# Sixteen-row loads in three buffers, and the last store ahead of the waits for all other transfers, in a row-mean kernel

## The chip, the core and the metric

The kernel runs on one core of a Trainium2 chip. The metric is the device time of one execution in microseconds (us). The span in a profile is shorter, by 1.6 us for the kernel before: it ends with the core's last instruction and leaves out the exit that follows. All runs told here have the state "fast" (none is over 1.5% above the fastest of its kernel), unless the text says otherwise, and the granted clock was 1.0 in every one.

## The reference

```python
x = randn(32, 512, 1024)            # float32, 64 MiB
out = np.sum(x, axis=-1) / 1024.0   # float32, 32 x 512
```

There are 16,384 rows of 4 KB, 128 per SBUF partition, each read once and reduced to one number.

## The kernel before

Rows are loaded in bulk by the sync engine (SP), summed by VectorE with some help from ScalarE, and scaled. The first 16 rows of each partition and the next 96 are scaled by GpSimd and stored; the last 16 are summed and scaled in small pieces, so that little is left to do when the last bytes land.

```python
    first = [(2, 0), (14, 0)]                      # rows of a load, rows of it on ScalarE
    main = [(14, 0)] * 5 + [(14, 4), (12, 5)]
    last = [(9, 4), (4, 2), (2, 1)]                # and one row in two halves, pa and pb
    ...
    bulk = ctx.enter_context(tc.tile_pool(name="bulk", bufs=3))
    ...
            t = bulk.tile([P, 14, D], F32, name="t")
            load(t[:, :rows, :], src[:, j : j + rows, :])
            ...
            nc.vector.reduce_sum(out=dst[:, j : j + d], in_=t[:, :d, :], axis=AX)
        ...
        nc.gpsimd.tensor_scalar_mul(out=dst, in0=dst, scalar1=scale)
    ...
    tc.keep_in_program_order(nc.sync.dma_start(out=o_main, in_=res))    # the large store, 96 rows
    ...
    dve_mean(fin[:, j:], pb)                                            # the last mean
    tc.keep_in_program_order(nc.sync.dma_start(out=o_last, in_=fin))    # the last store
```

After scheduling, a helper edits how the program closes. `drain` stands for the sync engine's waits for every transfer and engine, `end.instructions[1:-1]` for the closing barrier of all engines (two rounds; between them GpSimd clears the semaphores), and `last` for the wait for the last store's landing:

```python
    end.instructions = [
        with_sync(drain, on_wait=tuple(needs.values())),        # all but VectorE's last mean
        with_sync(store, on_wait=(done,), on_update=(add,)),    # VectorE's last mean
        *end.instructions[1:-1],
        with_sync(last, on_update=(sub,)),
    ]
```

## Time and profile before

| | before |
|---|---|
| median time, 6 runs | 160.75 us (160.63 to 160.82) |
| span of the profile | 159.1 us |
| DMA engines busy / VectorE busy | 98.2% / 74% |
| last half row lands | 157.13 us |
| last store issued / landed | 157.62 / 159.02 us |

The prediction shows the lines that give the bound (the last line of its first block, on the last store, stands in the view of DMA issues and not on the page). The timeline (start, duration, engine, line, operation) shows the last mean and the last store:

```profile
157.50 0.08 DVE L164 DVE_READ_ACCUMULATOR2_ANT fin<- 128x1 f32 x1
157.62 0.33 SPq L200 DMA_DIRECT2D out_dram<-fin  x1
```

The view of line L231, where the closing instructions stand, gives for each kind its count, its shortest, median and longest duration in ns, and its first and last start:

```profile
L231 SPq EVENT_SEMAPHORE  x7: 17/27/28, 155.9 to 158.8; - x7
L231 POOLq EVENT_SEMAPHORE  x4: 17/17/17, 158.2 to 158.7; - x4
...
L231 SPq DRAIN  x3: 7/7/129, 157.5 to 158.4; - x3
```

The sync engine begins its waits at 155.9, before the last store. GpSimd (POOLq) leads the barrier: it has everyone's first report at 158.2 and gives the last release at 158.7.

### The profile page before, as it was taken

The page shows a single profiled execution, that of the slowest core. Times are in us where ns is not written, and L with a number is a line of the kernel's source. Part 1 is how long each engine was busy: PE and PEld are TensorE (multiplying, and loading weights), DVE is VectorE, ACT ScalarE, POOL GpSimd, SP SyncE. Part 2 cuts the span into 40 slices and gives each one's busy share as a digit, 9 for nine tenths or more (in the row PEclk, how much of TensorE's full clock was granted, in tenths as well). Part 3 has the DMA queues.
Part 4 walks back from the last instruction along what each step waited for, and adds up shares of the span by engine and source line. Part 5 has one row for each costly group of instructions (what it writes and reads, how often), then busy time and mean ns, then how long its engine had stood idle before and what let it go on. Part 6 is the DMA issues. An engine that isn't in the chain of part 4 may idle for free.

```text
span 159.1 us, 147 instructions
## 1 busy us (share of the span) xinstructions
DVE 117.2 (74%) x29; ACT 18.5 (12%) x33; POOL 1.0 (1%) x7
## 2 busy tenths in 40 slices
DVE  0500059995999599977999599959995996395643
ACT  3000000000000000000000000000000900390684
POOL 0000000000000000000000000000000000001000
DMA  8999999979999999789999999699999999999894
GB/s 303 422 461 461 461 461 461 433 317 404 461 461 461 461 461 461 317 375 461 461 461 461 461 461 418 303 433 461 461 461 429 396 396 445 445 445 445 375 406 159
DMA packets 2448, 67.18 MB, mean 422 GB/s; under 512 B 656, under 2 KB 656, under 8 KB 912
## 3 DMA queue, kind: packets, MB, share of 16 engines
q1 hardware_dynamic: 2448, 67.18, 98.2%
HBM read 67.11 MB, written 0.07 MB: 422 GB/s over the span
## 4 chain that ended last, share of the span: by engine, by line
DMA 77%; DVE 21%; SPq 1%; issue 0%; DVEq 0%
DMA t<-in_x_dram 56%; DMA pb<-in_x_dram 21%; DVE res L177 20%; SPq L154 1%; DVE pb L164 0%; DVEq L231 0%
## 5 line engine op out<-in xcount | busy, mean ns | idle before, releaser
L177 DVE TENSOR_REDUCE res<-t 128x14 f32<-128x14336 f32 (+3 forms) x9 | 111.2, 12360 | 34.1 <-DMA t<-in_x_dram 34.1
L158 ACT ACTIVATE junk<-t 128x1024 f32<-128x1024 f32 x16 | 16.2, 1013 | 136.9 <-DMA t<-in_x_dram 136.9
L164 DVE CUSTOM_DVE_ANT_0 t<-t 128x512 f32<-128x512 f32 x8 | 5.1, 690 | 6.1 <-DMA t<-in_x_dram 6.1
L158 ACT ACTIVATION_READ_ACCUMULATOR junk<-t 128x1 f32 x16 | 3.0, 187 | 0.0
L179 POOL TENSOR_SCALAR res<-res 128x16 f32<-128x16 f32 (+1 forms) x2 | 0.7, 352 | 143.3 <-DVE res L177 143.3
L158 ACT ACT_TABLE_LOAD x1 | 1.3, 1283 | 1.7 <-PEq L217 1.7
L164 DVE DVE_READ_ACCUMULATOR2_ANT fin<- 128x1 f32 x9 | 0.8, 83 | 0.0
L164 DVE CUSTOM_DVE_ANT_0 pb<-pb 128x257 f32<-128x257 f32 x1 | 0.4, 428 | 0.2 <-DMA pb<-in_x_dram 0.2
L164 DVE CUSTOM_DVE_ANT_0 pa<-pa 128x256 f32<-128x256 f32 x1 | 0.4, 426 | 0.0
L151 POOL MEMSET pb<- 128x2 f32 x1 | 0.1, 99 | 1.3 <-POOLq L217 1.3
L217 POOL MEMSET const-bfloat16-1.0<- 128x1 bf16 x1 | 0.1, 102 | 0.0
L217 POOL MEMSET const-uint8-127<- 128x1 uint8 x1 | 0.1, 101 | 0.0
L217 POOL MEMSET const-float32-0.0<- 128x1 f32 x1 | 0.1, 98 | 0.2 <-issue 0.2
L217 POOL MEMSET const-float32-1.0<- 128x1 f32 x1 | 0.1, 98 | 0.0
L164 DVE DVE_READ_ACCUMULATOR2_ANT pb<- 128x1 f32 x1 | 0.1, 84 | 0.0
## 6 DMA issues: line engine op xcount, KB each, us to landing
t<-in_x_dram SPq DMA_DIRECT2D x7, 7168.0 KB, 35.6
t<-in_x_dram SPq DMA_DIRECT2D x1, 6144.0 KB, 33.3
t<-in_x_dram SPq DMA_DIRECT2D x1, 4608.0 KB, 27.2
t<-in_x_dram SPq DMA_DIRECT2D x2, 1024.0 KB, 19.2
t<-in_x_dram SPq DMA_DIRECT2D x1, 2048.0 KB, 31.7
pa<-in_x_dram SPq DMA_DIRECT2D x1, 256.0 KB, 33.9
pb<-in_x_dram SPq DMA_DIRECT2D x1, 256.0 KB, 33.9
out_dram<-res SPq DMA_DIRECT2D x1, 48.0 KB, 11.6
```

What stands on the lines that cost most here:

```text
L151: nc.gpsimd.memset(pb[:, D - c :], 0.0)
L154: tc.keep_in_program_order(nc.sync.dma_start(out=dst, in_=src))
L158: nc.scalar.activation(junk, src, COPY, scale=by, accum_out=dst)
L164: nc.vector.tensor_tensor_reduce(out=src[:, :h], in0=src[:, :h], in1=src[:, h:], scale=by, scalar=0.0, op0=ADD, op1=ADD, accum_out=dst,)
L177: nc.vector.reduce_sum(out=dst[:, j : j + d], in_=t[:, :d, :], axis=AX)
L179: nc.gpsimd.tensor_scalar_mul(out=dst, in0=dst, scalar1=scale)
L217: nc = _bacc.Bacc("TRN2", target_bir_lowering=False, num_devices=1)
```

## The change

Its intent: fewer and larger loads (64 KB a partition instead of 56), so one load fewer, with a four-row tile given up to make room for three larger buffers; and a last store that waits for nothing but its own data, its lane (the semaphore that its landing would raise in the scheduled program, shared with an earlier transfer) and the engines that make it, with the waits for everything else behind it.

```diff
     end.instructions = [
+        with_sync(store, on_wait=store.sync_info.on_wait, on_update=(add,)),
         with_sync(drain, on_wait=tuple(needs.values())),
-        with_sync(store, on_wait=(done,), on_update=(add,)),
         *end.instructions[1:-1],
 ...
-    main = [(14, 0)] * 5 + [(14, 4), (12, 5)]
+    main = [(16, 0)] * 4 + [(16, 4), (16, 7)]
 ...
-    t4 = one.tile([P, 4, D], F32, name="t4")
     t2 = one.tile([P, 2, D], F32, name="t2")
-    pa = one.tile([P, 768], F32, name="pa")[:, :c]
+    pa = one.tile([P, c], F32, name="pa")
 ...
-            t = bulk.tile([P, 14, D], F32, name="t")
+            t = bulk.tile([P, 16, D], F32, name="t")
 ...
-        t = bulk.tile([P, 14, D], F32, name="t")[:, :rows, :] if rows > 4 else t4 if rows == 4 else t2
+        t = t2 if rows == 2 else bulk.tile([P, 16, D], F32, name="t")[:, :rows, :]
```

## The prediction

> **What bounds the kernel now.** I read the page first, then the groups by shape, the timeline, the chain of waits and the sync engine's own waits. The page says which engine has no room:
>
> ```profile
> DVE 117.2 (74%) x29; ACT 18.5 (12%) x33; POOL 1.0 (1%) x7
> ...
> q1 hardware_dynamic: 2448, 67.18, 98.2%
> ...
> out_dram<-res SPq DMA_DIRECT2D x1, 48.0 KB, 11.6
> ...
> out_dram<-fin SPq DMA_DIRECT2D x1, 8.0 KB, 1.4
> ```
>
> VectorE is idle for a quarter of the span, while the 16 DMA engines hold packets for 98.2% of it. The page's row of GB/s jumps between 303 and 461; I don't read that as stalls, since a slice is some 4 us and one 56 KB packet takes 2.1 us, so a slice is credited with one packet per engine more or less. The landings tell the rate better, and in the timeline each reduction starts when its load has landed:
>
> ```profile
> 21.60 15.09 DVE L177 TENSOR_REDUCE res<-t 128x14 f32<-128x14336 f32 x1 [14.60 <-DMA t<-in_x_dram]
> ...
> 38.51 15.09 DVE L177 TENSOR_REDUCE res<-t 128x14 f32<-128x14336 f32 x1 [1.83 <-DMA t<-in_x_dram]
> ...
> 106.19 15.09 DVE L177 TENSOR_REDUCE res<-t 128x14 f32<-128x14336 f32 x1 [1.83 <-DMA t<-in_x_dram]
> ...
> 123.15 10.82 DVE L177 TENSOR_REDUCE res<-t 128x10 f32<-128x10240 f32 x1 [1.87 <-DMA t<-in_x_dram]
> ...
> 137.71 7.62 DVE L177 TENSOR_REDUCE res<-t 128x7 f32<-128x7168 f32 x1 [3.75 <-DMA t<-in_x_dram]
> ```
>
> From 38.51 to 123.15 there are five loads of 14 rows (7,168 KB, 7,340,032 bytes): 84.64 / 5 = 16.93 us each, 433.6 GB/s. VectorE waits about 1.8 us before each. A late buffer would show as a longer gap between two landings, and there is none. The chain of waits in order of time shows how it ends:
>
> ```profile
> 106.19 15.10 DVE res L177
> ...
> 121.30 0.33 SPq L154
> ...
> 123.19 33.94 DMA pb<-in_x_dram
> ...
> 157.15 0.43 DVE pb L164
> ```
>
> The 15.10 us of VectorE in that chain are there because a load's issue waited for a buffer, not because the DMA ran dry: the load issued at 121.30 queued behind one that landed at 137.71. So the bound is bytes through the DMA engines, plus a tail after the last half row has landed at 157.13: 0.45 us of VectorE, a store issued at 157.62, 1.4 us to its landing, span 159.1. The sync engine's waits give the tail's slack:
>
> ```profile
> SPq L231 <- DMA pa<-in_x_dram: 0.6, 1, 0.6
> ...
> SPq L231 <- DMA pb<-in_x_dram: 0.6, 1, 0.6
> ...
> SPq L87 <- SPq L87: 0.3, 1, 0.3
> ```
>
> The first two are waits ahead of the last store. The third is the final wait for that store's landing: only 0.3 us, so the closing barrier (L231), which runs while the store is in flight, is nearly as long as the store itself.
>
> **What the Trainium skill says.** Three places bear on it. "DMA: Bandwidth & Descriptors", section "Where 436 GB/s comes from", gives 435.2 GB/s for the 16 ports; the 433.6 found here is 99.6% of it, so there is almost nothing to win. "HBM Reference", section "Specifications (TRN2)", says that a core streaming alone gets about 425 GB/s rather than its half of the pair's 716; this trace agrees, slightly above. The first page's section "Anatomy of one DMA" gives a fixed cost of about 2.0 us per DMA (for the GpSimd path). Here that holds only for a transfer that someone waits for (1.4 us for the last store). For a load with another behind it the trace disagrees: 7,340,032 bytes at 435.2 GB/s are 16.87 us, and a load takes 16.93, so 0.06 us is all that comes on top.
>
> **The change part by part.** *One load fewer.* The packet records in the trace have one packet per partition row of a load, eight per engine: 57,344 bytes take 2,116 ns, 36,864 bytes 1,364 ns, 8,192 bytes 309 ns. From the first and the last, the slope is 1,807 / 49,152 = 0.03676 ns a byte (27.2 GB/s an engine, 435 for 16) and the rest is 309 - 301.2 = 7.8 ns per packet. The bytes stay. The 96 main rows go in six loads instead of seven, so eight packets per engine vanish: 8 x 7.8 = 62 ns. I estimate a 64 KB packet at 65,536 x 0.03676 + 7.8 = 2,417 ns and a 16-row load at 8 x 2,417 = 19.34 us. The saving is on the path: -0.06 us.
>
> *Do the larger buffers still arrive in time?* Loads land at 21.6, then each 19.34 us: 40.9, 60.3, 79.6, 98.9, 118.3, 137.6; nine rows, 10.85 us, 148.5; four, 4.86, 153.4; two, 2.50, 155.9; the halves, 157.07. A reduction over 16 rows: 14 take 15.085 and 7 take 7.620 us, so 1.066 a row and 0.16 fixed, 17.2 us, below 19.34. The load landing at 98.9 needs the buffer of that from 40.9: free at 58.1, while one load that lands at 60.3 and another at 79.6 are still queued, 21 us in hand. The four-row load, now in a bulk buffer, waits for the load of 118.3: VectorE's 12 rows take 12.95 us, to 131.2 (ScalarE's four rows are done by 122.5). It is issued there instead of at 121.7, and the pieces behind it wait too, but the queue holds the loads that land at 137.6 and 148.5, 17 us of work. So nothing is starved. VectorE's nine rows of the load from 137.6 end at 147.4 (7.62 + 2 x 1.066 = 9.75), 1.1 us ahead of the next landing. The large store follows GpSimd's 0.45 us at 147.9, 2 us later than now, and still queues behind the last halves. Path cost: 0.
>
> *The store ahead of the waits.* Before, the sync engine's waits for everything else end with the large store's landing, 145.89 + 11.6 = 157.49, and VectorE ends at 157.58. So these waits were already over, narrowly, when the last mean came, and the store was released by VectorE at 157.62. Gain: 0. In the built program the new store still waits for VectorE itself, its other two waits in one instruction ahead. But five wait instructions and a drain now run after the store's issue and before the closing barrier. In the trace neighbouring instructions of this kind start 40 to 75 ns apart, so the barrier moves by 0.24 to 0.4 us, against the 0.3 us of slack. In the span this costs 0 to 0.1 us. The measured time has 1.6 us more than the span (160.74 against 159.1), which I can't see inside; if the other engines' exits start that, it might grow by up to 0.3. I put +0.1 in all for this part.
>
> Sum: 160.74 - 0.06 + 0 + 0.1 = 160.8 us.
>
> **The rivals.** First, that each load carries a real fixed cost: with the skill's 2.0 us one load fewer would save 1.2%, to 158.8. The even 16.93 us between landings speaks against it; for it only that the chain has VectorE's 15.10 us in it. Second, that three larger buffers starve the queue: if the four-row load, issued at 131.2, were late, or 64 KB packets ran slower than the slope says, time would grow by what the queue idles; 17 us in hand speak against the first, and nothing in this trace has a 64 KB packet to test the second. If such a packet were cut in two, 6 x 8 x 7.8 = 0.37 us come on top, 161.2. Third, that the store was held by the waits: the margin of 0.1 us (157.49 against 157.58) is thin, and with a release by VectorE alone up to 0.1 us could be won in runs where the landing comes later, 160.65. Fourth, that the moved waits lengthen the exit fully: 0.4 us, 161.1.
>
> **Range and chances.** The terms I trust add up to a tenth; the exit term moves between -0.1 and +0.4, and two sets of runs may differ by some 0.2 us. That gives 160.4 to 161.2. A change of 2% is 3.2 us, 50 times the saving; it needs a slower packet rate or a starved queue. Faster 0.01, same 0.98, slower 0.01.
>
> **What would show it.** Right: landings of 16-row loads 19.3 us apart, 2,417 ns a packet, VectorE waiting some 2.1 us before each; the last half landing at 157.05 to 157.1; the last store issued 0.05 us after VectorE's end; the final wait (now 0.3 us) shrunk to nearly nothing. Wrong: landings further apart than 19.4 us, a gap between the nine-row and the four-row landing above 4.9 us, or a store issued clearly earlier after VectorE's end than now.

## The result, and the profile after

| | before | after |
|---|---|---|
| median time, 6 runs each | 160.75 us | 161.02 us (160.91 to 161.06) |
| span of the profile | 159.1 us | 159.2 us |
| last half row lands | 157.13 us | 157.20 us |
| last store issued / landed | 157.62 / 159.02 us | 157.69 / 159.08 us |

The ratio of after to before is 1.0017, 95% interval 1.0004 to 1.0029. Here and below a ratio is the mean time of one kernel's fast runs over that of the other's of the same rounds, so not quite the ratio of the medians. The change is within 2%, and 0.27 us slower by the medians.

The page of the changed kernel, the rows that answer to those of before (packets, MB and share of the DMA engines; for a store, KB and us from issue to landing):

```profile
DVE 115.0 (72%) x28; ACT 20.5 (13%) x37; POOL 1.0 (1%) x7
...
q1 hardware_dynamic: 2304, 67.18, 98.1%
...
out_dram<-res SPq DMA_DIRECT2D x1, 48.0 KB, 9.5
```

There are 144 packets fewer (128 for the load, and 16 four-byte ones, one per engine), the bytes are the same, and the engines are as full as they were. The reductions in the timeline:

```profile
40.95 17.22 DVE L177 TENSOR_REDUCE res<-t 128x16 f32<-128x16384 f32 x1 [4.26 <-DMA t<-in_x_dram]
...
118.32 12.95 DVE L177 TENSOR_REDUCE res<-t 128x12 f32<-128x12288 f32 x1 [2.13 <-DMA t<-in_x_dram]
...
137.75 9.76 DVE L177 TENSOR_REDUCE res<-t 128x9 f32<-128x9216 f32 x1 [6.47 <-DMA t<-in_x_dram]
```

Five loads land between 40.95 and 137.75: 19.36 us each, where the prediction had 19.34. The trace's packet records have a median of 2,418 ns for 64 KB, against 2,417 in the prediction. The chain of waits in order of time ends like this:

```profile
118.32 12.96 DVE res L177
...
131.30 0.33 SPq L154
...
132.66 24.54 DMA pb<-in_x_dram
...
157.22 0.43 DVE pb L164
```

The last loads are issued ten microseconds later than before (131.3 against 121.3), and the last half row lands all the same at 157.20. So the streaming part went as expected. The sync engine's own waits, the last store in the timeline and the closing line:

```profile
SPq L200 <- ACT junk L158: 8.6, 1, 8.6
SPq L200 <- DVE fin L164: 0.6, 1, 0.6
```

```profile
157.57 0.08 DVE L164 DVE_READ_ACCUMULATOR2_ANT fin<- 128x1 f32 x1
157.69 0.33 SPq L200 DMA_DIRECT2D out_dram<-fin  x1
```

```profile
L231 SPq EVENT_SEMAPHORE  x7: 17/28/28, 158.1 to 159.1; - x7
L231 POOLq EVENT_SEMAPHORE  x4: 17/17/17, 158.5 to 159.0; - x4
...
L231 SPq DRAIN  x3: 7/7/7, 158.4 to 158.7; - x3
```

The store now waits for ScalarE and VectorE alone, as intended, but it is issued no sooner after the last mean: 0.12 us from the start of that mean's last instruction, in both. What moved is the sync engine's waits: they begin at 158.1, behind the store, and with them the barrier. GpSimd has the first report at 158.5 instead of 158.2, and the last release comes at 159.0 instead of 158.7. The final wait for the landing, 0.3 us before (L87), is gone from the list.

The trace also records the semaphore events of the exit, past the span; the views don't print them, and I read them from the trace file. In the kernel before the first of these comes at 159.05 and the last at 160.72; in the changed one at 159.36 and 161.03. The first one comes 0.34 us after the barrier's last release in both. The sync engine's final wait, for the store's landing, ended at 159.05 in the kernel before, at the same moment, and at 159.16 in the changed one, 0.2 us earlier. So the barrier, and not the landing, seems to set off the exit. The Trainium skill, "Runtime: NRT & Kernel Launch", section "The ~15µs preamble/postamble breakdown", describes a barrier after the kernel that waits for all engines and, for the barrier ahead of the kernel, a chain across the engines with about 44 ns a hop; the trace of the exit agrees in kind: several of the gaps between these events are 0.034 to 0.047 us.

### The profile page after: what moved, and what is told of

The parts are those of the page before. It is cut to its first block, busy times and chain, and to the rows that moved or that the text cites. A ratio compares the mean times of both kernels' runs of the same rounds, so it can differ in the third digit from the quotient of the medians.

```text
span 159.2 us, 150 instructions
## 1 busy us (share of the span) xinstructions
DVE 115.0 (72%) x28; ACT 20.5 (13%) x37; POOL 1.0 (1%) x7
## 4 chain that ended last, share of the span: by engine, by line
DMA 66%; DVE 30%; another core or an unknown queue 1%; SPq 1%; issue 0%; DVEq 0%
DMA t<-in_x_dram 51%; DVE res L177 30%; DMA pb<-in_x_dram 15%; SPq L154 1%; DVE pb L164 0%; DVEq L231 0%
## 5 line engine op out<-in xcount | busy, mean ns | idle before, releaser
L177 DVE TENSOR_REDUCE res<-t 128x16 f32<-128x16384 f32 (+4 forms) x8 | 109.0, 13620 | 38.5 <-DMA t<-in_x_dram 38.5
L158 ACT ACTIVATE junk<-t 128x1024 f32<-128x1024 f32 x18 | 18.2, 1011 | 134.8 <-DMA t<-in_x_dram 134.8
```

Source lines behind the costliest of these rows:

```text
L158: nc.scalar.activation(junk, src, COPY, scale=by, accum_out=dst)
```

## The experiments

Three theories stood. Theory 1: the closing barrier sets the end, put off by the waits behind the store. Theory 2: the new loads cost the difference. Theory 3: the last store's landing sets the end.

The chips of the experiments were noisier than the first: where the kernel before ran 11 times beside one set, it took 160.54 to 161.29 us. Most of that scatter is in the stream of loads, as the spans show, which moved with the times. So I read the close in each trace from the landing of the last half row on:

| kernel (us after the last half row landed) | last store issued | it landed | barrier's last release | last event of the exit |
|---|---|---|---|---|
| before | 0.486 | 1.891 | 1.580 | 3.591 |
| new loads, old closing (two traces) | 0.540, 0.540 | 1.946, 1.949 | 1.637, 1.634 | 3.645, 3.643 |
| old loads, new closing (two traces) | 0.486, 0.487 | 1.884, 1.888 | 1.816, 1.818 | 3.825, 3.827 |
| after (two traces) | 0.487, 0.487 | 1.880, 1.896 | 1.824, 1.823 | 3.833, 3.832 |
| after, five more waits | 0.488 | 1.898 | 2.129 | 4.139 |
| report, then store | 0.625 | 2.023 | 1.242 | 3.506 |
| semaphore of its own | 0.619 | 2.029 | 1.235 | 3.502 |
| the same, large store's wait last | 0.501 | 1.916 | 1.127 | 3.388 |
| the same, old loads | 0.487 | 1.885 | 1.104 | 3.357 |

Where a kernel was traced twice, the last column agrees within 0.002 us, while the times differ by up to 0.3 us.

Two checks tie the last column to the measured times. In all 14 traces, the measured time of the traced execution is 0.11 to 0.13 us less than the moment of that last event, counted from the start of the span, so what moves that event moves the time. And the time less the span, for every execution, traced or not, is 1.51 to 1.60 us in all 43 with the old closing (31 of the kernel before, 12 of the new loads), 1.70 to 1.80 us in all 34 with the new closing and three buffers, and 1.27 to 1.37 us in all 21 of the last four rows. The three groups don't overlap, so the traces are not chance picks.

**New loads, old closing.**

```diff
     end.instructions = [
-        with_sync(store, on_wait=store.sync_info.on_wait, on_update=(add,)),
         with_sync(drain, on_wait=tuple(needs.values())),
+        with_sync(store, on_wait=(done,), on_update=(add,)),
```

> The loads of the changed kernel with the closing of the kernel before (the waits for everything else ahead of the last store). Theory 1 (the closing barrier, put off by the five waits and the drain behind the store, sets the end, and the loads are worth under 0.1 us): 160.75 us or 0.05 less, the same as the kernel before; the final wait for the store's landing is 0.3 us again. Theory 2 (the loads cost the 0.27 us, since the last half row landed 0.07 us later in the changed kernel's trace): 161.0 us, as the changed kernel.

Measured: 161.17 us against 160.82 on the same chip, ratio 1.0022 (1.0001 to 1.0043). Taken alone, this speaks for theory 2. But its six runs scatter from 160.71 to 161.61, and the trace puts the loss into the stream: packets of 56 KB that took up to 2,342 ns, where the first trace of the changed kernel has none above 2,122, and 64 KB packets of 2,428 ns on average against 2,421. The close is short again, 3.645 us. It isn't 3.591, because the waits held the store here: it was issued 0.081 us after VectorE's last mean instead of 0.028. With one load fewer the large store, which lands last of all others (158.03), is waited for one instruction earlier in the sync engine's list, and so one more instruction follows it.

Again on another chip:

> The new loads with the old closing again, since the first chip's times for it scattered over 0.9 us (its packets were slower, whatever the closing). Theory 1, with what the first trace of it showed (the waits hold the last store by 0.055 us, since the large store's semaphore is waited for one instruction earlier): 160.75 to 160.85 us, 3.645 us from the last half row to the last event. Theory 2 (the loads cost 0.27 us): 161.0 us.

Measured: 160.87 against 160.68 us, ratio 1.0016 (1.0002 to 1.0029), and 3.643 us for the close. The time lies between the two theories and just above theory 1's range; the close agrees with theory 1.

**Old loads, new closing.** The edit of the change in the closing list alone, on the kernel before.

> The loads of the kernel before with the closing of the changed kernel (store first, waits behind it). Theory 1: 161.0 to 161.1 us, 0.3 more than the kernel before, with the barrier's last release some 0.3 us later while the store is issued within 0.02 us of where it was before. Theory 2: 160.75 us.

Measured: 161.04 against 160.82 us, ratio 1.0013 (0.9996 to 1.0031), close 3.825 us. Again:

> The old loads with the new closing again, on the same chip: theory 1: 0.24 us more than the kernel before, 161.0 us, 3.825 us from the last half row to the last event. Theory 2: 160.75 us.

Measured: 161.06 against 160.68 us, ratio 1.0024 (1.0008 to 1.0040), close 3.827 us. The new closing alone makes the close 0.235 us longer (3.826 - 3.591), with the store issued at the same distance. That is theory 1.

**Five more waits.**

```diff
+    extra = [nc.sync.wait_ge(landed, 16).ins for _ in range(5)]
+    again = tuple(needs.values())[:2]                 # waits satisfied long ago
     end.instructions = [
         with_sync(store, on_wait=store.sync_info.on_wait, on_update=(add,)),
         with_sync(drain, on_wait=tuple(needs.values())),
+        *[with_sync(e, on_wait=again, on_update=()) for e in extra],
```

> The changed kernel with five more waits, each long satisfied, between the last store and the closing barrier. In the changed kernel's trace five such waits and a drain started 158.07, 158.13, 158.19, 158.25, 158.31, 158.38: 0.062 us apart. Theory 1: five more cost 5 x 0.062 = 0.31 us, 161.33 us. Theory 3 (the end is set by the last store's landing and the waits hide beside it): 161.0 us, as the changed kernel.

Measured: 161.30 against 160.82 us, ratio 1.0041 (1.0018 to 1.0065). The views of the added line and of the closing line (L235 in this kernel):

```profile
L90 SPq EVENT_SEMAPHORE  x5: 28/28/28, 158.4 to 158.7; - x5
```

```profile
L235 POOLq EVENT_SEMAPHORE  x4: 17/17/17, 158.8 to 159.3; - x4
```

Each wait executes in 0.028 us but starts 0.062 us after the one before. The barrier's last release moved from 159.0 to 159.3, and the close from 3.833 to 4.139 us: 0.306, against 0.31 expected. The store landed where it did before (1.898), so theory 3 falls for these kernels.

**Report to the barrier, then store.** What if the barrier comes earlier?

```diff
-    del needs[done.id]
+    needs = {done.id: needs.pop(done.id), **needs}    # wait for the last mean here
...
     end.instructions = [
-        with_sync(store, on_wait=store.sync_info.on_wait, on_update=(add,)),
         with_sync(drain, on_wait=tuple(needs.values())),
-        *end.instructions[1:-1],
+        *rest[:at],                                   # up to the sync engine's first report
+        with_sync(store, on_wait=(), on_update=(add,)),
+        *rest[at:],
```

> The loads of the changed kernel; the sync engine waits for everything, VectorE's last mean included, reports to the closing barrier, and only then issues the last store. The store is issued about 0.12 us later than in the kernel before, the barrier's last release about 0.2 us earlier. Theory 1 (the barrier sets the end): 160.55 us. Theory 3 (the store's landing sets the end): 160.85 us.

Measured: 161.04 against 160.82 us, ratio 1.0008 (0.9987 to 1.0029), which decides nothing: the last half row landed at 157.95 in its trace, 0.75 us later than after. The trace decides. The sync engine's final wait, and the barrier:

```profile
SPq L88 <- SPq L88: 0.8, 1, 0.8
```

```profile
L237 POOLq EVENT_SEMAPHORE  x4: 17/17/17, 158.5 to 159.2; - x4
```

The release comes 1.242 us after the last half row instead of 1.580, but the exit is only 0.085 us earlier (3.506). Neither theory 1 nor theory 3 is right alone: a gap inside the exit, 0.023 us in all kernels so far, is 0.333 us here, and ends 0.17 us after the last store landed. I read this as the exit waiting for the sync engine now, and that one for the landing. So the end is the later of two things: the barrier's release plus 2.01 us (before, after, and all of their variants above), or the landing plus 1.48 us (here; 1.47 in the three versions below). This rule fits all 14 traces within 0.01 us; what inside the exit waits for what is inferred from it.

**Quarter loads: the price of one load.**

```diff
-            load(t[:, :rows, :], src[:, j : j + rows, :])
+            for q in range(0, rows, 4 if rows == 16 else rows):
+                e = min(q + 4, rows) if rows == 16 else rows
+                load(t[:, q:e, :], src[:, j + q : j + e, :])
```

> The changed kernel with each of its six 16-row loads issued as four loads of 4 rows into the same buffer: 18 loads and 18 x 8 = 144 packets per DMA engine more, the same bytes. Theory 1 (a queued load costs only its packets, 7.8 ns each): 144 x 7.8 = 1.1 us more than the changed kernel, about 162.1 us; 0.7 us if packets overlap by the 3 ns that their records show. Rival (a load has a fixed cost of some 2 us that the queue doesn't hide): 36 us more, 197 us.

Measured: 161.54 us, where the changed kernel on the same chip took 160.92 and the kernel before 160.82 (ratio to before 1.0039, 1.0026 to 1.0053). The close is 3.826 us, as in the changed kernel, so the difference is in the stream. The 18 more loads cost 0.62 us, 0.034 us a load or 4.3 ns for each of 144 packets per engine. That is below both of my numbers and 60 times below the 2 us of the rival.

**Two buffers.**

```diff
-    bulk = ctx.enter_context(tc.tile_pool(name="bulk", bufs=3))
+    bulk = ctx.enter_context(tc.tile_pool(name="bulk", bufs=2))
```

> The changed kernel with two bulk buffers instead of three. A load is then issued when VectorE is done with the load before last, 2.1 us (19.34 - 17.2) before the queue runs dry; the first load's first packet started 1.02 us after its issue. Theory 1 (the queue is never short with three buffers and not even with two): within 0.3 us of the changed kernel. Rival (buffers and queue depth matter here): some 1 us or more for each of the five or six bulk loads that come late, 166 us or more.

Measured: 164.64 us in one run; three others, slow by the rule of 1.5% above the fastest, took 167.67 to 168.96. Before was 160.82. My expectation failed: the margin of 2.1 us is not enough, and the third buffer earned 3.7 us in that run against the changed kernel's 160.92. The profile is of a slow run, so I take from it only what may be the reason, not a size. Its page and its timeline:

```profile
q1 hardware_dynamic: 2304, 67.18, 95.8%
```

```profile
60.56 17.22 DVE L177 TENSOR_REDUCE res<-t 128x16 f32<-128x16384 f32 x1 [2.26 <-DMA t<-in_x_dram]
82.43 17.22 DVE L177 TENSOR_REDUCE res<-t 128x16 f32<-128x16384 f32 x1 [4.65 <-DMA t<-in_x_dram]
```

These two landings are 21.9 us apart instead of 19.4. The second load was issued at 58.33, 2.2 us ahead of the first one's landing; its packets started on the first engine at 59.84 but on the last at 61.91, and its first 16 took 2,727 ns on average. Why the fast run lost 3.7 us stays open.

**The changed kernel again**, as a base on that chip.

> The changed kernel once more, to compare the others of this call with it on the same chip: 161.0 us, and 3.83 us from the landing of the last half row to the last semaphore event of the exit, as in its first trace (the kernel before: 3.59).

Measured: 160.92 against 160.82 us, ratio 1.0003 (0.9990 to 1.0016). The time is nearer to before than the first time; since the close is 3.832 us, as in its first trace, that difference lies in the stream.

**A version meant to beat both.** The barrier should come early without the store coming late. The last mean gets a semaphore of its own, which the barrier does not clear; the sync engine waits for all else, reports, and then stores as soon as that semaphore allows.

```diff
+    body.instructions = [                             # the last mean signals `ready`, not VectorE's counter
+        with_sync(i, on_update=(dataclasses.replace(up, **here),)) if i.name == mean.name else i
+        for i in body.instructions
+    ]
...
     end.instructions = [
-        with_sync(store, on_wait=store.sync_info.on_wait, on_update=(add,)),
         with_sync(drain, on_wait=tuple(needs.values())),
-        *end.instructions[1:-1],
+        *rest[:at],                                   # up to the sync engine's first report
+        with_sync(store, on_wait=(dataclasses.replace(done, wait_value=1, **here),), on_update=(add,)),
+        *rest[at:],
+        with_sync(taken, on_update=(dataclasses.replace(sub, update_value=1, **here),)),
```

> A version that should beat both: the changed kernel's loads; the sync engine's waits for all transfers and its report to the closing barrier come ahead of the last store, and the store waits for VectorE's last mean on a semaphore of its own, which the barrier does not clear. In the run before, where the report came ahead of the store, the barrier was early and the landing of the store (1.48 us from it to the last event) set the end. Here the store should be issued 0.49 us after the last half row's landing, as in the kernel before, and land 1.9 us after it. Theory 1 with the landing as the next limit: 1.9 + 1.48 = 3.38 us from the last half row's landing to the last event, 0.2 less than before and 0.45 less than after: 160.55 us where the kernel before takes 160.75. Rival (the barrier has no say): 3.6 us as before.

Measured: 160.62 against 160.82 us, ratio 0.9985 (0.9972 to 0.9997); the changed kernel took 160.92 beside it, and its fastest run, 160.79, is above the slowest of this one, 160.75. The close is 3.502 us, not 3.38: the store was issued at 0.619, because four sync-engine instructions stood between the large store's landing and it. So the next version moves that one wait to the end of the list:

```diff
     del needs[done.id]
+    needs = {slow.id: needs.pop(slow.id), **needs}    # the large store's semaphore last
```

> The version with the semaphore of its own, and the wait for the large store, which lands last, moved to the end of the sync engine's waits, so that two instructions instead of four stand between that landing and the last store. In the run before, the last store was issued 0.28 us after the large store's landing (157.83 against 157.55) and so 0.13 us later than VectorE allowed. Theory 1 with the last store's landing (1.475 us to the last event) as the limit: store 0.49 us after the last half row, 3.37 us from that to the last event, 160.5 us. Rival (the barrier or something else is the limit by now): 3.5 us, 160.6 us as the version before.

Measured: 160.57 against 160.68 us, ratio 0.9992 (0.9980 to 1.0004), close 3.388 us. Its waits and its barrier:

```profile
SPq L91 <- SPq L91: 0.7, 1, 0.7
```

```profile
L249 POOLq EVENT_SEMAPHORE  x4: 17/17/17, 157.7 to 158.3; - x4
```

The barrier is over at 158.3, and the final wait for the landing is 0.7 us: the landing is the limit. In the trace this closes 0.20 us sooner than before and 0.445 sooner than after; in time the advantage over before is not clear of noise on this chip.

The same closing with the loads of before:

> The same closing with the loads of the kernel before (14 rows). From the run with quarter loads one load is worth 0.62 / 18 = 0.034 us: 0.03 us slower than the version with 16 rows, not to be told apart in time. Rival (the 16-row loads are what costs): 0.2 us faster.

Measured: 160.51 against 160.68 us, ratio 0.9989 (0.9977 to 1.0001), close 3.357 us. It is as fast as the version with 16 rows (160.57), so the larger loads neither win nor cost anything that these runs can tell. Its advantage over before, too, is not clear of noise.

**All runs together on theory 2.** Subtract from each kernel's difference to the kernel before (medians) the difference of its close, as in the table. What is left belongs to the stream. For the eight sets with 16-row loads in three buffers (quarter loads aside) it is -0.14 to +0.31 us, mean 0.07; for the three with 14-row loads -0.01 to +0.14, mean 0.06. With a scatter of 0.45 us between sets, no difference by the loads can be seen, and one of under some 0.1 us is not ruled out.

## Why the prediction was right

It said 160.8 us, 160.4 to 161.2, and the time was 161.02, in the same class. But its sum gave a change of +0.04 us, and the measured one is +0.27: the range held it because it left room for the exit, not because the sum was right. Step by step:

- *The bound.* Right. The DMA engines are as full as before, and the time of a 64 KB packet and the pace of the loads came out within 0.1%. Two of its signs were set too tight: of the five gaps between landings, two are 19.41 and 19.43 us, past its limit of 19.4, and the last half row landed at 157.20, not at 157.05 to 157.1.
- *One load fewer, -0.06 us.* The sign is right by the quarter loads, the size was too large: 0.034 us. The step that erred is "the rest is 7.8 ns per packet": consecutive packets' records overlap by about 3 ns, so a record's length is not what a packet adds. In the change itself the saving drowns: the last half row landed 0.07 us later in the first trace, not earlier, and across the traces between 157.13 and 157.95.
- *Larger buffers in time.* Right to 0.2 us: the four-row load was issued at 131.3 (131.2), the nine rows ended at 147.5 (147.4), the large store went at 148.06 (147.9). What "17 us in hand" is worth shows with two buffers, where 2 us in hand were not enough.
- *The store ahead of the waits, gain 0.* Right for the kernel as it was: 0.486 and 0.487 us after the last half row. But I priced it against the old loads. With the new ones the old closing would have held the store by 0.054 us (0.540), so within the combination the move brought the store forward by that much. It gained nothing at the end, which follows the barrier: with the new loads the close went from 3.644 to 3.833 us, 0.19 us longer.
- *The waits behind the store.* "The barrier moves by 0.24 to 0.4 us": it moved by 0.244, but by two steps of which the prediction had one. The five waits and the drain put the report off by 0.365 us, and the report itself, 0.129 us before, took 0.007. (Six steps of 40 to 75 ns are 0.24 to 0.45 us, so the range in the text was also cut a little short.) That the low end fits is luck.
- *The exit.* This term was mis-sized. I took 0.3 us of slack at the final wait for slack of the end, and "+0.1 in all" for a guess at what could not be seen. The five more waits show that the end follows the barrier one for one, so the whole 0.24 us counts. The span, which grew by 0.1 us, hides this.

Of the rivals, the fixed cost per load and the starved queue fell. The fourth, the moved waits lengthening the exit fully, was the right one, at 0.24 instead of 0.4 us. The third, the store held by the waits, holds for the new loads alone.

The sum with measured terms: -0.03 for the load, 0 for the buffers, +0.24 for the close, 0.21 us; the measured 0.27 differs by less than the stream's scatter.

## What to carry to other kernels

Moving a wait off the path of the last store pays only if the store was held by it; look for the time between the producer's end and the store's issue first. What an engine executes after its last useful instruction still counts when a closing barrier waits for it: here the end was the later of the barrier's release plus 2.01 us and the last store's landing plus 1.48 us, and the best closing brought the barrier forward without putting the landing off (1.885 us after the last half row, 1.891 before). When changes are of the size of the run's noise, measure the close from a fixed event in the trace, here the last load's landing, instead of comparing times.

## What the Trainium skill lacked or had wrong

- "DMA: Bandwidth & Descriptors", section "Anatomy of one DMA": about 2.0 us fixed for each DMA, for the GpSimd path. The section does not say what one load more costs behind others in a full queue: 0.034 us here for a load issued by the sync engine (18 more loads, 0.62 us). The last store, which nothing hid, took 1.4 us to land.
- The same page, section "Specifications": about 0.6 us to the first byte for loads issued by the sync engine. The first packet of the kernel started 1.02 us after the first issue, and the page does not say how far ahead of a queue's end a load must be issued: 2.2 us were too little with two buffers, where the first engine started 1.5 and the last 3.6 us after the issue (in a run of state slow).
- "Runtime: NRT & Kernel Launch", section "The ~15µs preamble/postamble breakdown": it gives the stages after the kernel, the first of which waits for all engines, but not how long after the kernel's own closing barrier or last landing the end comes. Here it came 2.01 us after the closing barrier's last release, or 1.48 us after the last store's landing where that was later.
- No page I found gives the price of a satisfied wait on the sync engine; it would belong to "Advanced Engine Details and Errata", section "Network/Comms", beside the time of reading a semaphore. A wait here executes in 0.028 us but the next starts 0.062 us later (five more waits cost 0.306 us).
